# A 4-layer float32 encoder trunk: evictions, squares and a gate's transfer change their place in the heads of the sub-layers

## The chip, the cores and the metric

One Trainium2 chip, 1 core. The metric is the device time of one launch in microseconds, as the median of repeated runs. TensorE has two clock levels, 1.2 and 2.4 GHz; the profile shows which share of the full one was granted.

## The reference, cut to what matters

The input x has 256 tokens of 1024 features, float32. Four layers follow; each has a token mixer (layers 0 and 3: latent attention, called MLA here; layer 1: a convolution module, conv; layer 2: causal pooling) and a squared-ReLU MLP. Every one of these eight sub-layers is wrapped in the same way:

```python
mod = c_act @ ada_w[i] + ada_b[i]
sh_m, sc_m, gt_m, sh_f, sc_f, gt_f = jnp.split(mod, 6, axis=-1)
h = _rmsnorm(x, norm_g[i, 0]) * (1.0 + sc_m[:, None]) + sh_m[:, None]
y = mixer(h)
x = x + gt_m[:, None] * _rmsnorm(y, norm_g[i, 1])
h = _rmsnorm(x, norm_g[i, 2]) * (1.0 + sc_f[:, None]) + sh_f[:, None]
y = jnp.square(jax.nn.relu(h @ w1)) @ w2
x = x + gt_f[:, None] * _rmsnorm(y, norm_g[i, 3])
```

What lies between two sub-layers is called a head here: y of the old one is normed, multiplied by its gate and added to x (the residual), and x is normed, scaled, shifted and transposed for the new one. A head bears the name of the sub-layer that follows it.

## The kernel before

**Work and numbers.** The 256 tokens are two tiles of 128 partitions (tile 0 and tile 1); x stays in SBUF as `xs`. Float32 products are made of three products in the rounded type float32r: a value is split into a high part (ScalarE, a cast) and a low part (VectorE, value less high part), and high x high, high x low and low x high are summed in PSUM. Weights are streamed by SP's queue into five buffers `raw` and split by `load` (lines 160 to 176: the cast on line 173, the subtraction on line 174), activations into two planes `hT`, high and low. The adaLN products `c_act @ ada_w` are spread over the whole kernel in units of a megabyte; `ada` (line 204) issues them on TensorE (line 271, eight matmul records a unit) or as accumulations on VectorE. A finished group becomes a row in `rows`, is staged in DRAM, and is sent back by POOL as a copy on all partitions (`spread`, line 330, the transfer on line 331, 512 KB): `bc_g` is the gate, `bc_a` the scales of the next sub-layer. `gate_row` (line 344) sends a mixer's gate, once for a layer.

**The order of work.** SP's transfers run in the order of the code. All other engines get their order from a planner, which goes by the order of the code, by estimated durations and by what is ready. Instructions that pass through `line(engine, ...)` (line 127) are chained on their engine in just the order in which the code makes them; `after` (line 147) puts the loads that follow a head behind the last instruction of that head on their engine. What passes through neither, such as the loads' casts and subtractions elsewhere, is set by the planner.

**A head** is `boundary` (lines 536 to 599). In the order of the code, each step in line on its engine: TensorE's pending adaLN units (`ada(units)`; from MLP 0's head to MLP 3's there are 1, 1, 2, 4, 1, 0 and 0 of them), squares of y of tile 0 (ScalarE, line 135), the two multiplications of y by the gate (`y_scaled`, VectorE, line 528), sum and power -1/2 of the mean (POOL, lines 119 and 121), residual (line 533), squares of the new x, and its scaling by `bc_a` (`scaled`, line 389). Then for tile 0 `transposed0`: a diagonal of the inverse norm (`dg`, ScalarE, line 403), and for each of two halves of the features one product that lays down the shift (line 395) and transposing products (line 409) into one PSUM bank. Meanwhile tile 1 gets its squares of y, multiplications by the gate, sum on VectorE (line 117), power on POOL, and residual. `fill0` evicts the two banks of tile 0 (lines 571 to 577): the cast into the high plane on ScalarE (line 573), the subtraction into the low plane on VectorE (line 574). Both casts stand in ScalarE's line ahead of tile 1's squares (line 581). Then `first(0)`, tile 0 of the next sub-layer's first block of weights, runs on TensorE (24 matmuls on line 645 in an MLP or in conv, 12 on line 836 in MLA) while tile 1's inverse norm is made; `transposed1` scales tile 1 (`xa`, VectorE, line 420), transposes it (TensorE, line 426), and evicts it in eight pieces (lines 429 and 431). Tile 1 of the first block follows, then chunk 1 of the MLP (line 671).

`headblock` (line 631) makes the first block for an MLP and for conv; its two halves of weights are loaded ahead of the head in the code. It goes through the high plane of all eight feature blocks first, with high and low weights (16 matmuls), and then through the low plane (8). The first half of the features is in the first bank of `fill0`, the second half in the second.

**Pooling** (lines 1266 to 1370) calls the same `boundary` with its own pieces: `tokens` (line 1287) in place of the transposes, and `early` (line 1343), which is called twice: after tile 1's multiplications by the gate, for the means of tile 0, and after tile 1's power. After the head come the rest of its product, `gate_row(i)` and `prep(i, 2)`, which send its own gate and the scales of MLP 2, and at the end one adaLN unit. The subtractions on line 1320 make the low plane of its means; the product on line 1330 needs it. The gate that is sent here is used in the next head, MLP 2's, on line 528.

Of the kernel before, what the change touches and what calls it, by code (L numbers as in the profile page):

```python
# [11 lines left out]
F32 = mybir.dt.float32  # L12
# [4 lines left out]
ALU = mybir.AluOpType  # L17
# [34 lines left out]
def tile_trunk(ctx: ExitStack, tc: tile.TileContext, x, cT, pos, invf, ada_w, ada_bg,  # L52
# [104 lines left out]

    loaded = {}

    def load(src, pre=None, lined=False):  # L160
        key = (src.tensor.name, src.offset)
        if key in loaded:
            return loaded.pop(key)
        o = (slice(0, src.shape[0]), slice(0, src.shape[1]))
        if key not in fetched:
            fetch(src)
        raw = fetched.pop(key)
        if pre is not None:
            pre(raw)
        h = his.tile([P, D], F32R, tag="hi", name="hi")[o]  # L170
        l = los.tile([P, D], F32R, tag="lo", name="lo")[o]
        put = (lambda ins, eng: line(eng, ins)) if lined else after
        put(A.copy(h, raw), "act")  # L173
        put(V.tensor_tensor(l, raw, h.bitcast(F32), op=ALU.subtract), "dve")  # L174
        gate["free"] -= 1
        return h, l

# [355 lines left out]
            line("dve", V.scalar_tensor_tensor(xs[:, t, sl], v, r, xs[:, t, sl],  # L533
                                               op0=ALU.mult, op1=ALU.add))

    def boundary(ys, units, planes=None, tokens=None, early=None, first=None):
        defer[0] = []
        ada(units)
        late, defer[0] = defer[0], None
        last.clear()  # L540
        final = planes is None and tokens is None
        m0, m1 = [sm.tile([P, 2], F32, tag="msy", name="msy") for _ in range(NT)]
        y_squares(0, ys, 0, m0)
        y_squares(0, ys, 1, m0)
        v0 = [y_scaled(0, ys, h) for h in range(2)]
        residual(0, v0, rsqrt_eps(*cols(m0)))
        if final:
            nc.sync.dma_start(out[0], xs[:, 0])
        else:
            ms = squares(0)  # L550
            xa = scaled(0)
        y_squares(1, ys, 0, m1)
        if not final:
            r = rsqrt_eps(*cols(ms))
            if tokens is None:
                bs = transposed0(xa, r)
        v1 = [y_scaled(1, ys, 0)]
        if tokens is not None:
            tokens(xa, r)
        y_squares(1, ys, 1, m1)  # L560
        r1 = rsqrt_eps(*cols(m1), eng=V)
        v1.append(y_scaled(1, ys, 1))
        if tokens is not None:
            low = early()
        if final:
            for v in v1:
                residual(1, [v], r1)
                nc.sync.dma_start(out[1, :, v[0]], xs[:, 1, v[0]])
            return

        def fill0(h):
            o = (slice(None), slice(4 * h, 4 * h + 4), slice(0, P))
            line("act", A.copy(planes[0][o], bs[h]))
            return lambda: line("dve", V.tensor_tensor(
                planes[1][o], bs[h], planes[0][o].bitcast(F32), op=ALU.subtract))
        if tokens is None:
            low = [fill0(h) for h in range(2)]
        residual(1, v1, r1)
        if tokens is not None:
            low[0][0]()  # L580
        ms = squares(1)
        r = rsqrt_eps(*cols(ms))
        if tokens is not None:
            low[1][0]()
            early()
            xa = scaled(1)
            low[0][1]()
            tokens(xa, r)
            low[1][1]()
        else:  # L590
            for l in low:
                l()
            if first is not None:
                first(0)
            transposed1(r, *planes)
        for a in late:
            ada_row(*a, line)
        gate["pool"] = gate["pow"]
        gate["free"] = GFREE if first is None else 0
# [28 lines left out]

    def headblock(src, hh, hl):
        parts = [load(src[p]) for p in range(2)]
        banks = []

        def tile_of(t):
            ts = slice(t * P, (t + 1) * P)
            b = bank("h", "h0")[:, 0:256]
            banks.append(b)
            n = 0
            for low in (False, True):  # L640
                for kk in range(KT):
                    wh, wl = parts[kk // 4]
                    c = slice(256 * (kk % 4), 256 * (kk % 4) + 256)
                    for st, mv in ((hl, wh),) if low else ((hh, wh), (hh, wl)):
                        line("pe", T.matmul(b, st[:, kk, ts], mv[:, c], start=(n == 0),  # L645
                                            stop=(n == 3 * KT - 1), skip_group_check=True))
                        n += 1
        return tile_of, banks
# [617 lines left out]
    def pool(i, head, consts, units, ahead):  # L1266
# [75 lines left out]

        def early():
            if not spilt:
                parts = [means(0, h) for h in range(2)]
                spilt.append(spill(0))
                return parts
            y.extend(y_banks())
            biased(0)
            product(0, 0)  # L1350
# [10 lines left out]
        for _, low in parts:  # L1361
            low()
        gate["free"] = 0
        gate_row(i)
        prep(i, 2)
        biased(1)
        product(1, 0)
# [24 lines left out]
    for s in range(nsub + 1):  # L1392
# [6 lines left out]

        if s == nsub:  # L1400
            boundary(y, 0)
        elif m == 0 and i % 3 == 2:
            y = pool(i, head, consts, sched[0], sched[2])
            pp.close()
        else:
            hi, lo = planes()
            first = None
            if m or i % 3 == 1:
                first = headblock(w1[i, 0] if m else w_pw1[i // 3, 0], hi, lo)
            elif s:  # L1410
                run = downblock(w_dkv[i // 3], hi, lo)
                first = [lambda t: run(t, (0, 1, 2, 3)), run]
            if s == 0:
                start(hi, lo)
                small_loads()
            else:
                head(planes=(hi, lo), first=first and first[0])
            if m:
                if i % 3 == 1:
                    pp = ExitStack()  # L1420
                    pool_p = pp.enter_context(tc.tile_pool(name=f"pool{i + 1}", bufs=1))
                    consts = pool_consts(pool_p, (i + 1) // 3)

                def mid():
                    if i + 1 < DEPTH:
                        prep(i + 1, 0)
                        if (i + 1) % 3 != 2:
                            shift_rows()
                    if i % 3 == 1:
                        spread(consts[2], i + 1, 0, 0)  # L1430
                        shift_rows(rows[(i + 1, 2)])
                y = ffn(i, (hi, lo), sched[0], sched[2], mid, first)
            else:
                args = (i, (hi, lo), sched[0], sched[2])
                if i % 3 == 0:
                    y = mla(*args, first and first[1])
                else:
                    y = conv(*args, first)
# [93 lines left out]
```

## Time and profile before

| what | value |
|---|---|
| median of 3 runs | 1166.6 us (1164.24 to 1167.7) |
| the profiled execution's own time | 1165.46 us |
| its span, first to last instruction | 1163.7 us |
| granted TensorE clock, mean over the span | 0.985 |
| TensorE matmuls busy | 1116.9 us (96%) |
| VectorE busy | 860.2 us (74%) |
| ScalarE busy | 643.3 us (55%) |
| POOL busy | 55.8 us (5%) |
| SP's DMA queue, share of the 16 DMA engines | 66.5% |
| HBM traffic | 248 GB/s over the span |

A row of the profile names an engine (PE is TensorE, PEld its loading of weights, DVE VectorE, ACT ScalarE), the line of the kernel, the operation, and what it writes and reads. An engine that is busy is not always the one that limits; the views that follow show who waits for whom, and when. A timeline joins neighbouring instructions of the same line and tile into one row with their count; the number in brackets is the time for which the engine stood idle before the row, and what released it.

### The profile page before, as it was taken

What the parts mean: (1) busy time and instruction counts of PE and PEld (TensorE: products, weight loads), DVE (VectorE), ACT (ScalarE), POOL (GpSimd) and SP (SyncE); (2) the same over time, 40 slices, a digit from 0 to 9 for tenths busy, and PEclk for the clock granted to TensorE, in tenths of its full rate; (3) what the DMA queues carried; (4) which work ended last, traced back from release to release, by engine and by line L of the source; (5) the groups of instructions that cost most, each with busy time, mean ns of one, the idle gap of its engine ahead of it and who ended that gap; (6) DMA issues with size and microseconds to landing.
All of it is one profiled execution on the core that took longest, in us unless ns stands there. A gap on an engine that the chain in (4) does not pass through costs nothing.

```text
span 1163.7 us, 17551 instructions
## 1 busy us (share of the span) xinstructions
PE 1116.9 (96%) x6682; PEld 910.8 (78%) x6682; DVE 860.2 (74%) x1206; ACT 643.3 (55%) x1146; POOL 55.8 (5%) x129
## 2 busy tenths in 40 slices
PE   7899999999999989999999989999998899999997
PEld 4667778878877767888888768888877778888886
DVE  3789788889675656888876688888756986655554
ACT  3455566555654225655564555656556665655653
POOL 1000000000010001000000100000010001000000
PEclk8999999999999989999999989999998999999999
DMA  9877769987825894898877559988625522765650
GB/s 367 321 275 305 294 241 348 336 318 286 316 86 174 308 341 155 307 388 328 307 282 293 226 207 379 332 314 289 210 72 177 172 91 71 258 197 188 188 187 36
DMA packets 73388, 290.02 MB, mean 249 GB/s; under 512 B 9988, under 2 KB 15236, under 8 KB 61016
## 3 DMA queue, kind: packets, MB, share of 16 engines
q1 hardware_dynamic: 70488, 280.45, 66.5%
q0 software_dynamic: 2816, 8.46, 2.1%
q8 instruction: 52, 0.85, 0.3%
q14 instruction: 32, 0.26, 0.1%
HBM read 286.58 MB, written 2.29 MB: 248 GB/s over the span
## 4 chain that ended last, share of the span: by engine, by line
PE 79%; DVE 7%; DMA 6%; ACT 3%; issue 3%; POOL 2%; SPq 0%; POOLq 0%; DVEq 0%; ACTq 0%
PE h L671 19%; PE y L602 11%; PE y L605 11%; PE y L606 11%; PE h L674 10%; PE adap L271 2%; DMA raw<-in_w_pw_dram 2%; ACT junk L135 2%; PE dw_ps L1131 2%; PE s_ps L1043 1%; DVE lo L174 1%; PE h L645 1%; POOL r L121 1%; PE pw L625 1%; PE pw L619 1%
## 5 line engine op out<-in xcount | busy, mean ns | idle before, releaser
L174 DVE TENSOR_TENSOR lo<-raw,hi 128x1024 fp32r<-128x1024 f32 (+1 forms) x334 | 391.4, 1194 | 79.6 <-ACT hi L173 53.1
L173 ACT CAST hi<-raw 128x1024 fp32r<-128x1024 f32 (+1 forms) x334 | 333.8, 1029 | 67.4 <-PE y L606 32.1
L671 PE MATMUL h<-hT,hi 128*128 128x512 f32 x960 | 240.0, 391 | 0.0
L671 PEld LDWEIGHTS h<-hT,hi 128*128 128x128 f32 x960 | 175.9, 188 | 36.2 <-issue 2.5
L605 PE MATMUL y<-lo,gh 128*128 128x512 f32 x512 | 200.0, 391 | 0.1
L606 PE MATMUL y<-hi,gl 128*128 128x512 f32 x512 | 199.1, 390 | 0.0
L602 PE MATMUL y<-hi,gh 128*128 128x512 f32 x512 | 197.2, 393 | 1.4 <-ACT hi L173 1.4
L736 ACT COPY r<-h 128x256 f32<-128x256 f32 x120 | 44.6, 372 | 183.4 <-PE h L674 183.3
L674 PEld LDWEIGHTS h<-hT,lo 128*128 128x128 f32 x960 | 130.8, 190 | 11.5 <-issue 2.5
L223 DVE SCALAR_TENSOR_TENSOR acc<-araw,c_act,acc 128x1024 f32<-128x1024 f32 x110 | 135.8, 1280 | 0.6 <-DMA araw<-in_ada_w_dram 0.5
L674 PE MATMUL h<-hT,lo 128*128 128x256 f32 x960 | 135.0, 283 | 0.0
L606 PEld LDWEIGHTS y<-hi,gl 128*128 128x128 f32 x512 | 96.1, 188 | 21.0 <-DVE gl L742 0.6
L602 PEld LDWEIGHTS y<-hi,gh 128*128 128x128 f32 x512 | 95.6, 188 | 21.2 <-ACT hi L173 1.6
L605 PEld LDWEIGHTS y<-lo,gh 128*128 128x128 f32 x512 | 96.3, 188 | 20.3 <-issue 1.7
L737 DVE TENSOR_TENSOR r<-h,r 128x256 f32<-128x256 f32 x120 | 50.3, 421 | 44.6 <-ACT r L736 43.5
L742 DVE TENSOR_TENSOR gl<-r,gh 128x512 fp32r<-128x512 f32 x60 | 41.4, 691 | 39.5 <-ACT gh L741 39.1
L738 ACT ACTIVATE r<-r 128x512 f32<-128x512 f32 x60 | 38.0, 633 | 33.3 <-DVE r L737 33.0
L528 DVE TENSOR_TENSOR v<-y,bc_g 128x512 f32<-128x512 f32 x32 | 21.9, 688 | 27.0 <-ACT junk L135 20.3
L602 PE MATMUL y<-hi,hT 128*128 128x512 f32 x96 | 38.2, 399 | 1.3 <-DVE hT L1230 1.3
L739 ACT ACTIVATE r<-r 128x512 f32<-128x512 f32 x60 | 37.9, 632 | 1.6
L741 ACT CAST gh<-r 128x512 fp32r<-128x512 f32 x60 | 37.2, 621 | 1.7
L605 PE MATMUL y<-lo,hT 128*128 128x512 f32 x96 | 37.5, 391 | 0.0
(262 smaller groups left out, 1470.2 us busy)
## 6 DMA issues: line engine op xcount, KB each, us to landing
raw<-in_w_dram SPq DMA_DIRECT2D x256, 512.0 KB, 4.7
araw<-in_ada_w_dram SPq DMA_DIRECT2D x96, 1024.0 KB, 7.2
raw<-in_w_pw_dram SPq DMA_DIRECT2D x24, 512.0 KB, 7.5
raw<-in_w_o_dram SPq DMA_DIRECT2D x16, 512.0 KB, 4.4
u<-ud SPq DMA_DIRECT2D x32, 132.0 KB, 3.3
raw<-in_w_ukv_dram SPq DMA_DIRECT2D x8, 512.0 KB
bc_g<-rowd POOLq DMA_DIRECT2D x8, 512.0 KB, 4.2
bc_a<-rowd POOLq DMA_DIRECT2D x7, 512.0 KB, 8.0
```

The source lines that it names most:

```text
L173: put(A.copy(h, raw), "act")
L174: put(V.tensor_tensor(l, raw, h.bitcast(F32), op=ALU.subtract), "dve")
L223: V.scalar_tensor_tensor(acc, raw[:, sl], ck, acc, op0=ALU.mult, op1=ALU.add)
L602: mm = T.matmul(o, ah, bh, start=start, stop=False, skip_group_check=True)
L605: T.matmul(o, ah, bl, start=False, stop=False, skip_group_check=True)
L606: return T.matmul(o, al, bh, start=False, stop=stop, skip_group_check=True)
L671: T.matmul(b, w(0, kk), pair[:, :, kk], start=(kk == 0), stop=False, skip_group_check=True)
L674: T.matmul(b[:, 0:S], w(1, kk), pair[:, 0, kk], start=False, stop=(kk == KT - 1), skip_group_check=True)
L736: A.copy(rf, hb[:, S:])
L737: V.tensor_tensor(rf, hb[:, 0:S], rf, op=ALU.add)
L738: A.activation(r, r, AF.Relu)
L742: gli = V.tensor_tensor(gl, g2, gh.bitcast(F32), op=ALU.subtract)
```

## The change

In the six heads that are not pooling's, the second bank of tile 0 is evicted by VectorE (a copy) in place of ScalarE, and this copy stands in the code behind tile 1's squares, behind the residual in VectorE's line. Where the head has adaLN units, the first bank's subtraction goes ahead of it; in the other two heads (MLA of layer 3 and MLP 3) the copy goes first. In MLP 2's head alone, the two subtractions of the first block's weights are held back and put in VectorE's line behind the scaling of tile 0. In pooling, `gate_row(i)` moves from behind the head into the first call of `early`.

```diff
--- before.py
+++ after.py
@@ -157,7 +157,7 @@
 
     loaded = {}
 
-    def load(src, pre=None, lined=False):
+    def load(src, pre=None, lined=False, held=None):
         key = (src.tensor.name, src.offset)
         if key in loaded:
             return loaded.pop(key)
@@ -171,7 +171,12 @@
         l = los.tile([P, D], F32R, tag="lo", name="lo")[o]
         put = (lambda ins, eng: line(eng, ins)) if lined else after
         put(A.copy(h, raw), "act")
-        put(V.tensor_tensor(l, raw, h.bitcast(F32), op=ALU.subtract), "dve")
+        def rest():
+            return V.tensor_tensor(l, raw, h.bitcast(F32), op=ALU.subtract)
+        if held is None:
+            put(rest(), "dve")
+        else:
+            held.append(lambda: line("dve", rest()))
         gate["free"] -= 1
         return h, l
 
@@ -533,7 +538,7 @@
             line("dve", V.scalar_tensor_tensor(xs[:, t, sl], v, r, xs[:, t, sl],
                                                op0=ALU.mult, op1=ALU.add))
 
-    def boundary(ys, units, planes=None, tokens=None, early=None, first=None):
+    def boundary(ys, units, planes=None, tokens=None, early=None, first=None, held=()):
         defer[0] = []
         ada(units)
         late, defer[0] = defer[0], None
@@ -549,6 +554,8 @@
         else:
             ms = squares(0)
             xa = scaled(0)
+            for h in held:
+                h()
         y_squares(1, ys, 0, m1)
         if not final:
             r = rsqrt_eps(*cols(ms))
@@ -570,11 +577,14 @@
 
         def fill0(h):
             o = (slice(None), slice(4 * h, 4 * h + 4), slice(0, P))
-            line("act", A.copy(planes[0][o], bs[h]))
+            if h == 0:
+                line("act", A.copy(planes[0][o], bs[h]))
+            else:
+                line("dve", V.tensor_copy(planes[0][o], bs[h]))
             return lambda: line("dve", V.tensor_tensor(
                 planes[1][o], bs[h], planes[0][o].bitcast(F32), op=ALU.subtract))
         if tokens is None:
-            low = [fill0(h) for h in range(2)]
+            low = [fill0(0)]
         residual(1, v1, r1)
         if tokens is not None:
             low[0][0]()
@@ -588,6 +598,9 @@
             tokens(xa, r)
             low[1][1]()
         else:
+            if units:
+                low.pop(0)()
+            low.append(fill0(1))
             for l in low:
                 l()
             if first is not None:
@@ -628,8 +641,8 @@
 
 
 
-    def headblock(src, hh, hl):
-        parts = [load(src[p]) for p in range(2)]
+    def headblock(src, hh, hl, held=None):
+        parts = [load(src[p], held=held) for p in range(2)]
         banks = []
 
         def tile_of(t):
@@ -1342,6 +1355,7 @@
 
         def early():
             if not spilt:
+                gate_row(i)
                 parts = [means(0, h) for h in range(2)]
                 spilt.append(spill(0))
                 return parts
@@ -1361,7 +1375,6 @@
         for _, low in parts:
             low()
         gate["free"] = 0
-        gate_row(i)
         prep(i, 2)
         biased(1)
         product(1, 0)
@@ -1404,9 +1417,10 @@
             pp.close()
         else:
             hi, lo = planes()
-            first = None
+            first = held = None
             if m or i % 3 == 1:
-                first = headblock(w1[i, 0] if m else w_pw1[i // 3, 0], hi, lo)
+                held = [] if m and i % 3 == 2 else None
+                first = headblock(w1[i, 0] if m else w_pw1[i // 3, 0], hi, lo, held)
             elif s:
                 run = downblock(w_dkv[i // 3], hi, lo)
                 first = [lambda t: run(t, (0, 1, 2, 3)), run]
@@ -1414,7 +1428,7 @@
                 start(hi, lo)
                 small_loads()
             else:
-                head(planes=(hi, lo), first=first and first[0])
+                head(planes=(hi, lo), first=first and first[0], held=held or ())
             if m:
                 if i % 3 == 1:
                     pp = ExitStack()
```

## Rows read from the trace of the kernel before

**Rows 1.** Waits of TensorE, whole span: us in total, times, longest us.

```profile
PE hT_ps L426 <- DVE xa L420: 6.6, 11, 1.9
```

**Rows 2.** Timeline, TensorE, 654 to 690: start, us, what, [idle before <-releaser].

```profile
653.79 1.90 PE L271 MATMUL adap<-araw,c_act 128*32 128x512 f32 x16
...
670.48 1.33 PE L1330 MATMUL y<-hi,hT 128*128 128x256 f32 x8 [2.86 <-DVE hT L1320]
671.74 3.61 PE L271 MATMUL adap<-araw,c_act 128*32 128x512 f32 x16
...
677.12 1.16 PE L409 MATMUL hT_ps<-dg,xa 128*128 128x128 f32 x8 [1.36 <-ACT dg L403]
...
683.10 1.12 PE L645 MATMUL h<-hi,hT 128*128 128x256 f32 x8
...
688.93 1.41 PE L671 MATMUL h<-hT,hi 128*128 128x512 f32 x5
```

**Rows 3.** Timeline, VectorE, 654 to 690.

```profile
654.82 0.68 DVE L528 TENSOR_TENSOR v<-y,bc_g 128x512 f32<-128x512 f32 x1
...
668.54 1.29 DVE L528 TENSOR_TENSOR v<-y,bc_g 128x512 f32<-128x512 f32 x2 [6.67 <-DMA bc_g<-rowd]
669.74 1.28 DVE L1320 TENSOR_TENSOR hT<-pT_ps,hT 128x512 fp32r<-128x512 f32 x2
670.94 2.35 DVE L174 TENSOR_TENSOR lo<-raw,hi 128x1024 fp32r<-128x1024 f32 x2
673.21 1.41 DVE L533 SCALAR_TENSOR_TENSOR xs<-v,r,xs 128x512 f32<-128x512 f32 x2
...
678.55 1.41 DVE L533 SCALAR_TENSOR_TENSOR xs<-v,r,xs 128x512 f32<-128x512 f32 x2
```

**Rows 4.** Timeline, POOL, 654 to 690.

```profile
654.98 0.55 POOL L121 TENSOR_TENSOR r<-v,mhalf 128x1 f32<-128x1 f32 x1 [1.86 <-DVE v L117]
...
659.77 0.63 POOL L331 DMA_DIRECT2D bc_g<-rowd  x1
660.40 0.55 POOL L331 DMA_DIRECT2D bc_a<-rowd  x1
```

**Rows 5.** Line 331, whole span: its sends' time to landing.

```profile
DMA to landing us min/median/max: 3.8/5.3/10.5
```

**Rows 6.** Stretches: us, each engine's busy time, PEclk, DMA share, GB/s.

```profile
656.00:659.00 3.00, 3.00 (x25) 2.67 (x24) 2.79 (x5) 2.15 (x6) 0.13 (x1) 1.00 1.00 421
671.00:675.00 4.00, 4.00 (x22) 1.16 (x21) 4.00 (x6) 0.92 (x3) 0.00 (x0) 0.60 0.21 31
```

**Rows 7.** Timeline, ScalarE, 654 to 690.

```profile
663.92 0.19 ACT L135 ACTIVATION_READ_ACCUMULATOR junk<-y 128x1 f32 x1
...
674.05 0.63 ACT L135 ACTIVATE junk<-xs 128x512 bf16<-128x512 f32 x1 [6.66 <-DVE xs L533]
...
676.67 0.40 ACT L403 ACTIVATE dg<-ident,r 128x128 f32<-128x128 f32 x1 [0.42 <-POOL r L121]
```

**Rows 8.** Line 1067: xcount, ns min/median/max, first and last start, shape.

```profile
L1067 DVE COPY ptA<-pT_ps x8: 685/692/693, 83.1 to 955.2; 128x512 f32<-128x512 f32 x8
```

**Rows 9.** Timeline, MLP 3's head, ScalarE, VectorE, TensorE, 973 to 990.

```profile
977.78 0.59 ACT L573 CAST hT<-hT_ps 128x512 fp32r<-128x512 f32 x1 [0.91 <-PE hT_ps L409]
...
976.53 1.42 DVE L533 SCALAR_TENSOR_TENSOR xs<-v,r,xs 128x512 f32<-128x512 f32 x2
...
980.83 1.54 DVE L420 SCALAR_TENSOR_TENSOR xa<-xs,r,bc_a 128x256 f32<-128x256 f32 x3 [1.69 <-POOL r L121]
...
981.37 0.83 PE L426 MATMUL hT_ps<-ident,xa 128*128 128x128 f32 x4 [0.77 <-DVE xa L420]
...
985.93 2.09 PE L671 MATMUL h<-hT,hi 128*128 128x512 f32 x8
```

**Rows 10.** Timeline, TensorE, in the heads of conv and of MLA.

```profile
344.64 0.84 PE L426 MATMUL hT_ps<-ident,xa 128*128 128x128 f32 x4 [1.07 <-DVE xa L420]
...
872.57 0.88 PE L426 MATMUL hT_ps<-ident,xa 128*128 128x128 f32 x4 [1.91 <-DVE xa L420]
```

## The prediction

> **What bounds the kernel now.** The table of the page is read first: TensorE is busy 96% of the span, so a change pays only where TensorE itself stands still, or where a chain that it waits for gets shorter. Its waits come next: eleven for the scaled copy of the second tile, 6.6 us in all, the longest 1.9 [rows 1]; two in each of the six ordinary heads, one in MLP 2's. The third view is the timeline from pooling into MLP 2, where the largest hole is. TensorE stands 2.86 us before a product of pooling, and 1.36 before the transposes of the next head [rows 2]. VectorE stands 6.67 us before its first multiplication by the gate [rows 3]: the gate was sent at 659.77 [rows 4], and that multiplication starts 8.8 us after the send. The order on VectorE makes it worse: the two subtractions of pooling (L1320) for which TensorE waits stand behind the multiplications by the gate, and the residual stands behind two subtractions of weights, 2.35 us for the pair [rows 3]. From 671 to 675 the granted clock was 0.60 [rows 6], a mean between the two levels of 1.2 and 2.4 GHz, right after TensorE had stood; 16 accumulations took 3.61 us there against 1.90 at 653.79 [rows 2].
>
> **Part 1: pooling sends its gate from within its head.** The send now stands on POOL behind the power that ends at 655.53 [rows 4], and its buffer is free when the last multiplication by the old gate ends, at 655.50 [rows 3]. So it goes at 655.6 instead of 659.77. It holds POOL for 0.63 us [rows 4]; what stands behind it there is the second tile's sum and power, which wait for squares that come later, so nobody waits for POOL. On SP's queue nothing moves. On the DMA engines, full at that time (share 1.00, 421 GB/s [rows 6]), the gate's 512 KB go ahead of as much of other loads, which come 1.2 us later; the first that is used feeds the accumulations at 671.74. How long does the gate take? Line 331's sends took between 3.8 and 10.5 us [rows 5]; I take the 8.8 of this very one, since the engines are as full, and both ends for the range. The multiplications by the gate then start at 664.4. They could not start before 664.1, when the squares of y are through [rows 7], so a faster transfer is worth 0.3 us at most, and a slower one (10.5) costs 1.8.
>
> The Trainium skill (DMA: Bandwidth & Descriptors, Anatomy of one DMA) gives such a transfer 2.0 us plus its bytes at 436 GB/s, by estimate 3.2 us for 512 KB. The trace does not agree: 8.8 us beside full engines. By the page the gate would be there at 658.8, and the sum below would be the 0.3 us larger.
>
> From there each step keeps its distance. L1320 starts 1.2 us after the multiplications; its pair, 1.28, ends at 666.9 [rows 3]. TensorE reaches that product at 667.6, so its wait of 2.86 is gone, the product ends at 668.9, and the accumulations, at the full clock's 1.90, at 670.8 [rows 2].
>
> **Part 2: the subtractions of MLP 2's first weights are held.** They leave their place ahead of the residual. That now starts 1.2 us after L1320, at 666.8 instead of 673.21 [rows 3]: 6.4 us, of which 4.1 are the gate's and 2.3 the pair's. The first tile's diagonal follows 3.46 us later as it did (676.67 after 673.21 [rows 3, 7]), at 670.3. With one shift product of some 0.4 after 670.8 the transposes start at 671.2 instead of 677.12, without their wait. The pair now stands ahead of the second tile. The row of scales, sent at 659.8 (now 660.40 [rows 4]), is there by the same 8.8 at 668.6; the scaling by it (1.2), the pair (2.35), and the two multiplications by the gate (1.29) bring the second tile's residual to 673.5 instead of 678.55. The first matmul that needs the held subtractions comes after the transposes, and they end at 672.1 (now 673.3), so neither TensorE nor SP's next loads into those buffers wait longer.
>
> **Part 3: the second eviction goes to VectorE, in six heads.** On ScalarE it took 0.59 us [rows 9], and the second tile's squares stood behind it. No row shows VectorE copying from PSUM into the rounded type. The like copy of 128x512 from PSUM takes it 0.692 [rows 8]; I take 0.69, with ScalarE's 0.59 as the other end. On VectorE it stands behind the residual (1.42) and, in a head that has accumulations, behind the first subtraction too (0.64, half of the pair's 1.28). Who waits for it: 16 of the 24 matmuls of the first block's tile.
> - MLP 3. The squares could start 0.84 after the residual's start (as 674.05 after 673.21 [rows 3, 7]), at 977.4; now they follow the eviction that ends at 978.4 [rows 9]. The second half's square follows 0.75 behind the first, so the scaled copy comes 0.9 earlier, 979.9 instead of 980.83. But VectorE's copy ends at 978.6, ScalarE's at 978.4: the block's tile ends 0.2 later, at 980.8 (now 981.37 less the wait of 0.77 [rows 9]). The transposes follow at once. In MLP 2, where they do so today, chunk 1 begins 4.7 us after that tile's end (688.93 after 684.22 [rows 2]). So 985.5 instead of 985.93: 0.4 us.
> - MLA. TensorE waits 1.91 us [rows 10], and its first block uses the first half alone, so the copy delays nothing: 0.85, about MLP 3's 0.9.
> - Conv. The wait is 1.07 [rows 10]; an accumulation that stands ahead of the scaled copy takes part of it: 0.5.
> - MLP 0 and 1 have accumulations, so the copy comes 0.64 later and TensorE waits for it in place of the scaled copy: 0.2 each, between -0.4 and 0.8.
> - MLP 2. Residual from 673.5 to 674.9, subtraction, copy: 676.3. The other 16 matmuls take 2.1 (8 in 1.12 [rows 2]): 678.4. With 4.7 more, chunk 1 starts at 683.1 instead of 688.93: 5.8 us, for all three parts.
>
> **Sum.** 5.8 + 0.4 + 0.85 + 0.5 + 0.4 = 8.0 us. From the profiled execution's 1165.46 this gives 1157.5; that execution lies 1.1 below the median of the runs shown, so 1158.6. Behind the heads the MLPs go at TensorE's pace, so what a head gains stays. With the slow transfer 5.8 becomes 4.0; if the other heads lose 0.4 each, or all waits of rows 1 go, their 2.2 becomes -2.0 or some 5. Ends: 1164.6 and 1155.5.
>
> **Rivals.**
> - The heads give nothing: VectorE becomes what TensorE waits for. For it speaks that the copy ends later there in five heads; against it, that in MLA nothing else waits. Then pooling's 5.8 less up to 0.6 is left: 1161.
> - The gate lands late. A send of line 331 has taken 10.5 us [rows 5]. Mechanism: right behind the new send VectorE works without a pause on residual and scaling, and POOL's descriptors are written later. The gate is used from 666.2, L1320 ends at 668.7, and TensorE waits 1.1: 1.8 us are lost, 1160.4. The Trainium skill (SBUF — State Buffer, SBUF: two separate sides) says that VectorE's two-port modes keep POOL from writing descriptors; no run here shows whether such a mode is at work.
> - The gate does not go early: its issue stays where it is on POOL, because the planner so orders it. Then only the held pair pays, 2.3, and the heads up to 2.2: 1162 to 1164.5. Against it: from 655.53 on POOL has nothing to do before the second tile's sum.
> - Slower. The planner orders the unlisted casts, subtractions and accumulations by its own estimate of times. Moved heads may set a subtraction of weights ahead of what TensorE needs, on VectorE, in the stages behind the first head. Each place costs 1.2 us, half of the pair's 2.35 [rows 3]; of 64 chunks more than seven have to be hit before the gain is gone. With ten: 1170.
>
> **How the numbers follow.** The forecast's case has 0.58, the heads' rival 0.16, the late gate 0.08, the gate not early 0.12, slower 0.06. A measurement of this kernel can tell about 0.3%, 3.5 us, from no change. The first three are faster by more, and so is a quarter of the fourth, the rest of which lies within: 0.85, 0.09, 0.06. The range goes from 1155.0, all waits of the heads gone, to 1163.5, which takes in half of the fourth case.
>
> **What would show it.** The gate is sent at 655.6 and used at 664.4; TensorE does not wait at 667.6; the residual of MLP 2 starts at 666.8, its chunk 1 at 683.1 (earlier by what the heads before have gained). In the other heads the squares stand right behind the first eviction, and in place of the wait before the second transposes there are short waits for VectorE's copy. The prediction is wrong if the gate is used after 666, if a wait for the row of scales takes its place, or if chunk 1 in MLP 3 follows its head no sooner than today.

## The result and the profile after

The changed kernel takes 1158.72 us in the median (1156.78 to 1160.32, 5 runs), the kernel before 1165.72 on the same chip (1163.28 to 1167.70, 5 runs): ratio 0.9939, 95% interval 0.9920 to 0.9958. Measured twice more, it gave 0.9933 (0.9912 to 0.9954) and 0.9932 (0.9911 to 0.9954). The forecast was 1158.6, with a range of 1155.0 to 1163.5, and faster; so the total is right. Its parts are not: in the trace pooling's passage gave 2.58 us of the 5.8 that were forecast (some 70% in two later traces), the other heads twice as much as forecast.

In the profile after, TensorE's waits for the second tile's scaled copy are down from 6.6 us in eleven [rows 1] to 1.3 in four. The wait for the diagonal in MLP 2's head has grown from 1.36 [rows 2] to 2.05; the other of the two in the first row, some 0.6 in MLA's head, stood there before too. TensorE's waits from 140 to 1000 us (total, times, longest):

```profile
PE hT_ps L414 <- ACT dg L408: 2.7, 2, 2.1
...
PE hT_ps L431 <- DVE xa L425: 1.3, 4, 0.7
```

The passage from pooling into MLP 2 follows, engine by engine (timelines of the kernel after: start, us, what, idle before). First GpSimd, which answers to [rows 4]:

```profile
655.10 0.63 POOL L336 DMA_DIRECT2D bc_g<-rowd  x1 [0.27 <-DVE v L533]
...
669.45 1.58 POOL L119 TENSOR_SCALAR v<-ms 128x1 f32<-128x1 f32 x1 [4.99 <-ACT junk L135]
671.12 1.39 POOL L121 TENSOR_TENSOR r<-v,mhalf 128x1 f32<-128x1 f32 x1
```

VectorE, which answers to [rows 3]:

```profile
664.73 1.29 DVE L533 TENSOR_TENSOR v<-y,bc_g 128x512 f32<-128x512 f32 x2 [3.56 <-DMA bc_g<-rowd]
665.94 0.74 DVE L538 SCALAR_TENSOR_TENSOR xs<-v,r,xs 128x512 f32<-128x512 f32 x1
666.60 1.28 DVE L1333 TENSOR_TENSOR hT<-pT_ps,hT 128x512 fp32r<-128x512 f32 x2
667.80 0.74 DVE L538 SCALAR_TENSOR_TENSOR xs<-v,r,xs 128x512 f32<-128x512 f32 x1
668.52 1.29 DVE L394 TENSOR_TENSOR xa<-xs,bc_a 128x512 f32<-128x512 f32 x2
669.73 2.35 DVE L175 TENSOR_TENSOR lo<-raw,hi 128x1024 fp32r<-128x1024 f32 x2
```

And TensorE, which answers to [rows 2]:

```profile
667.34 1.33 PE L1343 MATMUL y<-hi,hT 128*128 128x256 f32 x8 [0.41 <-DVE hT L1333]
668.60 1.92 PE L276 MATMUL adap<-araw,c_act 128*32 128x512 f32 x16
...
672.99 1.97 PE L414 MATMUL hT_ps<-dg,xa 128*128 128x128 f32 x8 [2.05 <-ACT dg L408]
...
675.61 2.07 PE L414 MATMUL hT_ps<-dg,xa 128*128 128x128 f32 x8
...
685.66 1.56 PE L684 MATMUL h<-hT,hi 128*128 128x512 f32 x6
```

The gate does go early, the wait of 2.86 before pooling's product shrinks to 0.41, and the accumulations run at the full clock (1.92 where 3.61 stood). Then GpSimd's sum (line 119) and power (line 121) of the first tile take 1.58 and 1.39 us. In the kernel before they took 0.37 and 0.56:

```profile
675.62 0.37 POOL L119 TENSOR_SCALAR v<-ms 128x1 f32<-128x1 f32 x1 [10.46 <-ACT junk L135]
676.07 0.56 POOL L121 TENSOR_TENSOR r<-v,mhalf 128x1 f32<-128x1 f32 x1
```

The diagonal waits for them, TensorE for the diagonal, and behind that wait the clock falls: both groups of transposes take some 2 us, and the stretches from 674 on show half of the full clock (us, busy time by engine, granted clock, DMA share, GB/s):

```profile
674.00:676.00 2.00, 2.00 (x8) 1.34 (x8) 1.94 (x4) 1.01 (x2) 0.39 (x1) 0.50 1.01 414
676.00:678.00 2.00, 2.00 (x11) 2.00 (x11) 0.72 (x2) 0.92 (x4) 0.87 (x3) 0.50 0.85 346
678.00:680.00 2.00, 2.00 (x11) 2.00 (x11) 1.97 (x5) 0.00 (x0) 0.56 (x1) 0.51 0.32 82
```

The first chunk of MLP 2 comes at 685.66. From the start of the accumulations to it are 17.06 us, where the kernel before took 17.19 (688.93 less 671.74 [rows 2]): nearly all that was won lies ahead of them.

**Where the time went, head by head.** Each of TensorE's matmuls was set against the same one, in order of issue, in the trace of the kernel before; a passage's gain is the change, across it, of the median distance between the two starts. In us, for all kernels of this study:

| kernel | pooling to MLP 2 | MLP 0 | conv | MLP 1 | MLA | MLP 3 | five heads |
|---|---|---|---|---|---|---|---|
| forecast | 5.8 | 0.2 | 0.5 | 0.2 | 0.85 | 0.4 | 2.2 |
| after | 2.58 | 0.55 | 0.70 | 1.19 | 1.24 | 0.75 | 4.4 |
| after, again | 4.25 | 0.43 | 0.69 | 1.19 | 0.42 | 0.78 | 3.5 |
| after, third | 4.11 | 0.87 | 0.70 | 1.21 | 0.78 | 0.78 | 4.3 |
| gate only | 4.14 | -0.05 | 0.05 | 0.03 | 0.03 | 0.01 | 0.1 |
| eviction only | -0.49 | 0.48 | 0.70 | 1.20 | 1.06 | 0.78 | 4.2 |
| squares first | -0.23 | 0.73 | 0.96 | 0.97 | 0.88 | 0.38 | 3.9 |
| no held pair | 5.51 | 0.62 | 0.65 | 1.21 | 0.99 | 0.80 | 4.3 |
| held later | 5.66 | 0.88 | 0.70 | 1.20 | 0.85 | 0.78 | 4.4 |
| held later, again | 5.83 | 0.56 | 0.70 | 1.21 | 0.65 | 0.79 | 3.9 |
| PSUM work instead | 2.91 | 0.64 | 0.71 | 1.21 | 1.14 | 0.77 | 4.5 |
| later, ScalarE's copy | 6.09 | 0.57 | 0.68 | 1.21 | 0.86 | 0.79 | 4.1 |
| mixed | 5.97 | 0.34 | 0.97 | 1.21 | 1.04 | 0.79 | 4.4 |

Outside the heads single executions differ by as much. By 135 us every one of these runs is 1.4 to 5.0 us behind the profiled execution of the kernel before, and inside conv each gains 1.1 to 4.4, "gate only" 3.1 of it with conv's code untouched. Neither belongs to the change.

### The profile page after: what moved, and what is told of

Same layout as the page of the kernel before. It is cut to its first block, busy times and chain, and to the rows that moved or that the text cites. A ratio compares the mean times of both kernels' runs of the same rounds, so it can differ in the third digit from the quotient of the medians.

```text
span 1157.0 us, 17554 instructions
## 1 busy us (share of the span) xinstructions
PE 1114.3 (96%) x6682; PEld 913.4 (79%) x6682; DVE 864.2 (75%) x1212; ACT 639.2 (55%) x1140; POOL 58.4 (5%) x129
## 4 chain that ended last, share of the span: by engine, by line
PE 80%; DVE 6%; DMA 6%; ACT 3%; issue 2%; POOL 2%; SPq 0%; POOLq 0%; DVEq 0%; ACTq 0%
PE h L684 19%; PE y L615 11%; PE y L618 11%; PE y L619 11%; PE h L687 10%; PE adap L276 2%; PE h L658 2%; DMA raw<-in_w_pw_dram 2%; PE dw_ps L1144 1%; ACT junk L135 1%; PE s_ps L1056 1%; DVE lo L175 1%; POOL r L121 1%; PE pw L632 1%; PE pw L638 1%
## 5 line engine op out<-in xcount | busy, mean ns | idle before, releaser
L533 DVE TENSOR_TENSOR v<-y,bc_g 128x512 f32<-128x512 f32 x32 | 21.9, 688 | 22.4 <-ACT junk L135 18.7
```

## The experiments

In the passage into MLP 2 these are the numbers that tell the kernels apart (us, from the timelines; the last column runs from the start of the sixteen accumulations to that of the first chunk):

| kernel | GpSimd's sum | power | TensorE waits for the diagonal | transposes, 1st and 2nd group | to chunk 1 |
|---|---|---|---|---|---|
| before | 0.37 | 0.56 | 1.36 | 1.16, 2.07 | 17.19 |
| after | 1.58 | 1.39 | 2.05 | 1.97, 2.07 | 17.06 |
| after, again | 1.57 | 1.39 | 2.04 | 1.16, 2.08 | 15.52 |
| after, third | 1.67 | 1.39 | 2.15 | 1.16, 2.06 | 15.63 |
| gate only | 1.44 | 0.85 | 1.38 | 1.16, 2.07 | 15.66 |
| no held pair | 1.44 | 0.85 | 1.38 | 1.16, 1.16 | 14.02 |
| held later | 0.67 | 0.56 | 0.32 | 1.16, 1.16 | 14.15 |
| held later, again | 0.55 | 0.56 | under 0.3 | 1.16, 1.16 | 14.15 |
| PSUM work instead | 0.55 | 0.56 | 2.16 | 1.16, 1.99 | 16.84 |
| later, ScalarE's copy | 0.67 | 0.56 | 0.32 | 1.16, 1.16 | 13.81 |
| mixed | 0.50 | 0.56 | under 0.3 | 1.16, 1.16 | 13.80 |

**1. The early gate alone** (kernel before, lines of `pool`):

```diff
             if not spilt:
+                gate_row(i)
                 parts = [means(0, h) for h in range(2)]
...
         gate["free"] = 0
-        gate_row(i)
         prep(i, 2)
```

> The kernel before with pooling's gate sent from within its head, and nothing else. Theory A (after the change, GpSimd's sum and power for the diagonal took 1.58 and 1.39 us because the held pair of subtractions ran beside them, and this took back what holding the pair brought): VectorE does gate multiplication, eviction pair, weight pair, residual, scaling one behind the other from about 665.4, the diagonal starts near 673.7 where it was at 676.67, both GpSimd instructions take under 1 us together with 0.4, and the first chunk of MLP 2 comes 2.5 to 3.5 us earlier relative to the work ahead of it, about what the whole change gave there (2.6). Theory B (the held pair earned its 2.35 us as forecast, and the loss was elsewhere): the early gate alone gives 0.3 us or nothing. Total: A 1163 us, B 1165.5 us.

Measured: 1161.13 us, ratio 0.9959 (0.9943 to 0.9974). The passage gives 4.14 us, the two GpSimd instructions take 1.44 and 0.85, and the diagonal starts at 672.11. So the gate gave by itself what theory A gave it and 0.6 us beyond its range: the planner set the residual ahead of the weights' pair by itself, its first half even ahead of pooling's subtractions, so the diagonal came 1.6 us sooner than expected, though GpSimd's two instructions, expected under 1 us, were slow here too (the pair, not held, ran beside them). Theory B falls.

**2. The eviction and the squares alone** (the diff's lines in `fill0` and the four behind it, on the kernel before):

```diff
-            line("act", A.copy(planes[0][o], bs[h]))
+            if h == 0:
+                line("act", A.copy(planes[0][o], bs[h]))
+            else:
+                line("dve", V.tensor_copy(planes[0][o], bs[h]))
...
-            low = [fill0(h) for h in range(2)]
+            low = [fill0(0)]
...
+            if units:
+                low.pop(0)()
+            low.append(fill0(1))
```

> The kernel before with the second eviction on VectorE and the second tile's squares ahead of it in every head, the gate where it was. Theory A: what the heads gave after the change is theirs: TensorE's work moves up by 0.55 (MLP 0), 0.7 (conv), 1.2 (MLP 1), 1.1 (MLA) and 0.76 us (MLP 3), 4.3 in sum, and something between 0 and 1 us in MLP 2's head; total about 1161 us. Theory B (the forecast's own: 0.2, 0.5, 0.2, 0.85, 0.4): 2.2 us in sum, total 1163.5 us, the rest of the heads' gain after the change being chance of one profiled execution.

Measured: 1160.62 us, ratio 0.9947 (0.9931 to 0.9964). Head by head theory A's sizes repeat within 0.1, 4.2 us in all. In MLP 2's head, where 0 to 1 us of gain was expected, it loses 0.49; the clock was at the half level for about 10 us there, where the kernel before had about 7 (worked out from the mean clocks of the stretches, 655 to 685).

**3. The held pair one place later on VectorE** (kernel after):

```diff
             xa = scaled(0)
-            for h in held:
-                h()
...
         v1 = [y_scaled(1, ys, 0)]
+        for h in held:
+            h()
```

> The kernel after the change with the held pair one place later on VectorE, behind the multiplication of the second tile's first half by the gate. Theory A (GpSimd's instruction cannot run beside a VectorE instruction that reads two operands from SBUF): the sum takes 0.4 us instead of 1.58 and the power 0.6 to 1.0 instead of 1.39, the diagonal starts near 670.7 instead of 672.54, TensorE's wait of 2.05 us ahead of the transposing products falls under 0.4, and the first chunk of MLP 2 comes 1.5 to 3 us earlier than after the change; total 1156 to 1157.5 us. Theory B (the two GpSimd instructions are slow for another reason, such as the DMA issues or the clock): they still take 2.5 us or more together and the time stays at 1158.7 us.

Measured: 1156.11 us, ratio 0.9912 (0.9899 to 0.9925). GpSimd and VectorE in the timeline of this kernel:

```profile
669.09 0.67 POOL L119 TENSOR_SCALAR v<-ms 128x1 f32<-128x1 f32 x1 [4.83 <-ACT junk L135]
669.85 0.56 POOL L121 TENSOR_TENSOR r<-v,mhalf 128x1 f32<-128x1 f32 x1
```

```profile
668.30 1.29 DVE L394 TENSOR_TENSOR xa<-xs,bc_a 128x512 f32<-128x512 f32 x2
669.75 0.69 DVE L533 TENSOR_TENSOR v<-y,bc_g 128x512 f32<-128x512 f32 x1 [0.15 <-ACT junk L135]
670.36 2.35 DVE L175 TENSOR_TENSOR lo<-raw,hi 128x1024 fp32r<-128x1024 f32 x2
```

The same pair, 0.6 us later, and GpSimd is back to 0.67 and 0.56. The sum began at 669.09 (its time includes any wait beside VectorE) and ended at 669.77, 0.18 after the scaling (L394), whose two operands lie in SBUF, had ended at 669.59 (668.30 plus 1.29). The power ran beside L533, one of whose operands lies in PSUM, at its usual 0.56. TensorE:

```profile
670.89 1.16 PE L414 MATMUL hT_ps<-dg,xa 128*128 128x128 f32 x8 [0.32 <-ACT dg L408]
...
672.39 1.16 PE L414 MATMUL hT_ps<-dg,xa 128*128 128x128 f32 x8
676.16 0.39 PE L658 MATMUL h<-hi,hT 128*128 128x256 f32 x1 [1.66 <-DVE hT L583]
...
682.39 1.78 PE L684 MATMUL h<-hT,hi 128*128 128x512 f32 x7
```

No half clock, and chunk 1 is 5.66 us earlier than in the kernel before: the forecast's 5.8, without the delay. Theory A holds. A new wait shows, 1.66 us for VectorE's copy.

**4. PSUM work in the pair's place** (on the kernel of experiment 3; the results of the three multiplications are not used):

```diff
             xa = scaled(0)
+            if held:
+                v = tmp.tile([P, 512], F32, tag="v", name="v", bufs=3)
+                for h in (0, 1, 0):
+                    line("dve", V.tensor_tensor(v, ys[1][h], bct["g"][:, HALF[h]],
+                                                op=ALU.mult))
```

> As the kernel with the held pair later, but in the place the pair left stand three multiplications of 128x512 (2.1 us) with one operand in PSUM and one in SBUF, whose results are not used. Theory A (two SBUF operands on VectorE block GpSimd): the sum takes about 0.4 us and the power 0.57, the diagonal starts near 670.6. Theory B (any busy VectorE slows GpSimd): the two take 2.5 us or more together, as after the change. In both the second tile's residual is some 2 us later than with the pair moved.

It ran once (1159.45 us), so its time is not compared. GpSimd, VectorE and ScalarE in its timeline:

```profile
668.14 0.55 POOL L119 TENSOR_SCALAR v<-ms 128x1 f32<-128x1 f32 x1 [4.88 <-ACT junk L135]
668.77 0.56 POOL L121 TENSOR_TENSOR r<-v,mhalf 128x1 f32<-128x1 f32 x1
```

```profile
668.43 2.21 DVE L560 TENSOR_TENSOR v<-y,bc_g 128x512 f32<-128x512 f32 x3
```

```profile
670.75 0.60 ACT L135 ACTIVATE junk<-y 128x512 bf16<-128x512 f32 x1 [2.71 <-DVE v L560]
...
671.34 0.39 ACT L408 ACTIVATE dg<-ident,r 128x128 f32<-128x128 f32 x1
```

VectorE works without a pause from 668.43 to 670.64, and the power that runs beside it takes 0.56. A busy VectorE alone does not slow GpSimd; theory B falls. The diagonal missed its 670.6: the power was ready at 669.33, but the square of y that stands ahead of the diagonal on ScalarE waited 2.71 us for the added multiplications, which read the same PSUM tiles. That delay is this experiment's own.

**5. Held later, and in MLP 2's head the second copy on ScalarE, ahead of the squares:**

```diff
-            if h == 0:
+            if h == 0 or held:
                 line("act", A.copy(planes[0][o], bs[h]))
...
-            low = [fill0(0)]
+            low = [fill0(h) for h in range(2 if held else 1)]
...
-            if units:
-                low.pop(0)()
-            low.append(fill0(1))
+            if not held:
+                if units:
+                    low.pop(0)()
+                low.append(fill0(1))
```

> As the kernel with the held pair later, but in MLP 2's head alone both evictions of the first tile are on ScalarE again, ahead of the second tile's squares. Theory A (there ScalarE stands idle for 1.66 us when the second bank is ready at 673.55, while VectorE's copy has to wait behind the residual until 675.43): TensorE's wait of 1.7 us for VectorE's copy goes, the second tile's scaled copy becomes the limit, and the first chunk of MLP 2 comes 0.5 to 1 us earlier than with VectorE's copy; total about 1155.4 us. Theory B (the copy on VectorE is as good there as in the other heads): no change within 0.3 us or up to 0.7 us later, 1156.1 us or more.

Measured: 1155.84 us, ratio 0.9927 (0.9906 to 0.9949). From the accumulations to chunk 1 it takes 13.81 where experiment 3 took 14.15, a gain of 0.34. The wait of 1.66 for the copy is gone, but about half of it comes back as waits for the scaled copy (0.53 and 0.25 us), and the second tile's transposes, now in two groups, take 0.90 and 0.63 instead of 1.04. Between the two theories' sizes.

**6. After without the held pair:**

```diff
-                held = [] if m and i % 3 == 2 else None
```

> The kernel after the change without the held pair: the two subtractions stand where the planner puts them, between the residual and the scaling. Theory A (holding the pair back, where the change puts it, costs more than it brings, since it then runs beside GpSimd's power as well): the power takes 0.85 us instead of 1.39, the diagonal starts 0.3 to 0.6 us earlier and the first chunk of MLP 2 comes 0.5 to 1.2 us earlier than after the change; total 1157.5 to 1158.5 us. Theory B (the forecast's: holding the pair brings 2.3 us): the chunk comes 2 us later, total 1161 us.

Measured: 1155.38 us, ratio 0.9918 (0.9894 to 0.9942), with "after, again", measured together with it, at 1157.23; the intervals of the two ratios overlap. The planner puts the pair between residual and scaling, 668.70 to 671.05 in "gate only" and likewise here:

```profile
668.85 1.44 POOL L119 TENSOR_SCALAR v<-ms 128x1 f32<-128x1 f32 x1 [5.10 <-ACT junk L135]
670.37 0.85 POOL L121 TENSOR_TENSOR r<-v,mhalf 128x1 f32<-128x1 f32 x1
```

VectorE's rows beside them:

```profile
667.85 2.35 DVE L175 TENSOR_TENSOR lo<-raw,hi 128x1024 fp32r<-128x1024 f32 x2
670.12 1.28 DVE L394 TENSOR_TENSOR xa<-xs,bc_a 128x512 f32<-128x512 f32 x2
```

The sum is nearly as slow, the power less so, and TensorE waits 1.38 us instead of 2.05. The power stands beside the scaling alone, 128x512 with both operands in SBUF, and takes 0.85; beside experiment 4's multiplications, 128x512 too but with one operand in PSUM, it took 0.56. So it is not the length of VectorE's instruction that tells. Holding the pair back where the change holds it does not bring 2.3 us; it costs 0.7 (2.05 less 1.38), and in this execution the clock's fall as well. Theory A on the sign, beyond its range on the size (1.5 us to chunk 1 against "after, again"; 3.0 against the first trace). Against experiment 3 nothing is lost at chunk 1: 14.02 here, 14.15 there.

**7. Squares first, the copy stays on ScalarE behind them** (as experiment 2, without the copy on VectorE).

> The kernel before with the second tile's squares ahead of the second eviction, which stays on ScalarE, behind them. Theory A (the heads' gain comes from the squares going first, not from the engine of the copy): the five ordinary heads together gain as with the copy on VectorE, 4.2 us (0.5, 0.7, 1.2, 1.05, 0.78) within 1 us, total about 1161 us. Theory B (the copy must also leave ScalarE): the copy, now behind the squares, makes TensorE wait for it as long as it waited for the scaled copy; the heads gain under 2 us, total 1164 us or more.

Measured: 1160.33 us, ratio 0.9961 (0.9942 to 0.9981). The five heads give 3.9 us, against 4.2. It is the order that pays. The engine of the copy matters by head: VectorE's is better by 0.4 in MLP 3 and 0.2 in MLP 1, ScalarE's by 0.26 in conv.

**8. The kernel after, once more.**

> The kernel after the change, once more, as a yardstick beside the three others. Theory A (what differs between two profiled executions in the first 30 us and between 400 and 435 us is chance of the clock): the work up to 135 us is not 4.4 us later than in the kernel before, but anything between 0 and 5; the passage from pooling into MLP 2 and the heads repeat within 0.3 us, GpSimd's sum at 1.58 and its power at 1.39 us. Theory B (the change moves the start): the 4.4 us repeat. Total 1158.7 us within 1.5 in both.

Measured: 1157.23 us. GpSimd's two instructions repeat to 0.01, the wait is 2.04, but the passage gives 4.25 instead of 2.58, since the clock fell later and for less long; the start is 3.8 us behind that of the kernel before, where "eviction only" was 1.4 behind. MLA's head gave 0.42 instead of 1.24. So of theory A the 0.3 us does not hold for the passage and MLA's head. On the start 3.8 lies near theory B's 4.4 too; what decides is "gate only", 2.8 behind with the code ahead of pooling untouched.

**9. Mixed:** held later; the second copy on ScalarE behind the squares in MLP 0 and conv, on ScalarE ahead of them in MLP 2, on VectorE elsewhere (in the kernel of experiment 5, `h == 0 or units == 1`).

> The held pair later, and the second eviction by head: on ScalarE behind the squares in MLP 0 and conv, on ScalarE ahead of them in MLP 2, on VectorE in MLP 1, MLA and MLP 3 (each where the runs so far gave most). Theory A (the parts add up): pooling into MLP 2 gains 6 us or more against the kernel before, MLP 0 0.7, conv 0.95, MLP 1 1.2, MLA 0.9 to 1.1, MLP 3 0.78, 10.5 us in all; ratio near 0.991. Theory B (a head takes back what another gives, through the clock or the planner's order): under 9 us.

Measured: 1152.79 us, ratio 0.9902 (0.9871 to 0.9933), the lowest median of the study. In its trace the passage and the five heads give 5.97 and 4.35, 10.3 us together; MLP 0 gave 0.34 where 0.7 was expected. TensorE goes through the passage almost without a stand:

```profile
667.78 1.16 PE L414 MATMUL hT_ps<-dg,xa 128*128 128x128 f32 x8
...
669.28 1.16 PE L414 MATMUL hT_ps<-dg,xa 128*128 128x128 f32 x8
...
679.10 2.08 PE L685 MATMUL h<-hT,hi 128*128 128x512 f32 x8
```

**10 and 11. Held later and after, again.**

> The kernel with the held pair later, once more, beside the one after the change in the same call. Theory A (TensorE's wait ahead of the transposes stays under 0.5 us, and so the clock does not fall behind it): the sixteen accumulations to the first chunk of MLP 2 take 14.1 us again, 1.4 to 2.9 less than after the change, the granted clock is 1.00 all the way, and the median is 1 to 3 us below that of the kernel after the change. Theory B (the clock's fall there is chance whatever TensorE does): 15 to 17 us, and no difference in the medians.

> The kernel after the change for the third time. TensorE's wait for the diagonal is 2.0 to 2.1 us again, GpSimd's two instructions 1.6 and 1.4; by theory A the clock falls to 0.50 behind that wait again, for 3 to 6 us, and the accumulations to the first chunk take 15.5 to 17.1 us; by theory B it may as well not fall (14 us).

Measured together: 1155.67 us (0.9920, 0.9896 to 0.9944) and 1158.22 (0.9932). To chunk 1: 14.15, exactly as in experiment 3, and 15.63. The medians differ by 2.6 us, within theory A's 1 to 3, though the intervals of the ratios overlap, so by the times alone the difference is not shown. In three executions of the kernel after, the clock fell three times, and it was at half speed for about 7 us once and for 3.4 us twice (worked out from the mean clocks of the stretches); with the pair later it never did in two.

## Why the prediction was right in sum and wrong in parts

- **The gate.** It was sent as predicted. It was used 9.6 us after the send (664.73 less 655.10), not 8.8: between the value taken and the end kept for the range (10.5 [rows 5]). That is 0.8 of the 2.9 us by which the diagonal came late (next point). Pooling's subtractions started 1.87 us after the multiplications (666.60 less 664.73), not 1.2, since the planner set the first half of the residual between them; with the later gate that left 0.41 of TensorE's wait. The rival of the late gate happened by half.
- **The held pair: the step that failed.** "The first tile's diagonal follows 3.46 us later as it did (676.67 after 673.21 [rows 3, 7]), at 670.3." The stage runs 0.7 us ahead, so 669.6 was forecast, and 672.54 was measured. 3.46 was a distance across GpSimd, taken over from a place where VectorE did other work, and the pair was then put beside just those two instructions: 1.58 and 1.39 us instead of 0.37 and 0.56, 2.0 us. Experiment 3 moves only the pair and gets them back; experiment 4 shows that it is not VectorE's being busy. Where the pair stood next, and who ran beside it there, was not asked of the step that moved it. Nor were the pair's 2.3 us there to be won: once the gate is early, the planner sets the pair behind the residual by itself ("gate only", "no held pair"). Held later, the pair gives hardly more than not held: 5.66 and 5.83 against 5.51 in the passage, and 14.15 against 14.02 to chunk 1, since what the diagonal's wait gives (0.32 for 1.38) the wait for VectorE's copy takes back (1.66 for 0.49).
- **The mechanism.** Wherever the sum or the power is slow in this passage, it ends 0.1 to 0.5 us behind a VectorE instruction with both operands in SBUF: here the sum at 671.03, 0.1 after the pair's first half, the power at 672.51, 0.4 after the second. Beside multiplications that read PSUM it keeps its 0.3 to 0.6. The Trainium skill (SBUF — State Buffer, SBUF: two separate sides) says so: a VectorE instruction with two SBUF inputs and a GpSimd instruction that reads SBUF share a port pair that one of them holds for its whole instruction; the other is blocked. The trace agrees: 1.58 and 1.39 us beside the pair, 0.55 and 0.56 beside experiment 4's multiplications. The prediction took from that section only the sentence that bears on descriptors, and missed this one, which spoke against the pair's new place.
- **The clock.** The forecast had the transposes at 1.16 us, since TensorE would not stand. It stood 2.05, and the stretches behind show 0.50. That the stand brought the fall is argued from its place in time; the last section names stands that no fall followed. Three executions of one kernel lost different amounts by it (17.06, 15.52, 15.63 to chunk 1), so of the missing 3.2 us (5.8 less 2.58) some 1.5 are one execution's chance; the other two gave 4.25 and 4.11.
- **MLP 2's head.** The forecast counted the copy on VectorE as part of its gain. It costs 0.34 us, between experiments 3 and 5, both at the full clock. ScalarE stands idle there when the bank is ready (673.55 in experiment 3), while VectorE is at the residual and copies from 675.43. The 0.49 lost in experiment 2 cannot be put down to the copy, since the clock was at the half level longer there; squares first, with the copy on ScalarE, loses 0.23 as well.
- **The other heads: 2.2 forecast, 3.5 to 4.4 measured.** The squares did go first, and most of the waits went, from 6.6 us to 1.3. (They are two in each of five ordinary heads and one in MLP 2's; the prediction's "six" does not add up to eleven.) Two terms were too small, as MLP 1 shows. TensorE in the kernel before and in the one after:

```profile
469.68 1.12 PE L645 MATMUL h<-hi,hT 128*128 128x256 f32 x8
471.55 0.83 PE L426 MATMUL hT_ps<-ident,xa 128*128 128x128 f32 x4 [0.75 <-DVE xa L420]
472.61 0.66 PE L426 MATMUL hT_ps<-ident,xa 128*128 128x128 f32 x4 [0.22 <-DVE xa L420]
...
476.12 1.18 PE L671 MATMUL h<-hT,hi 128*128 128x512 f32 x4
```

```profile
470.28 1.12 PE L658 MATMUL h<-hi,hT 128*128 128x256 f32 x8
471.24 1.04 PE L431 MATMUL hT_ps<-ident,xa 128*128 128x128 f32 x8
...
475.46 1.77 PE L684 MATMUL h<-hT,hi 128*128 128x512 f32 x7
```

From the end of the tile's products to chunk 1 it is 5.32 us before (476.12 less 470.80) and 4.06 after (475.46 less 471.40); the forecast took 4.7, MLP 2's of before, where the transposes too went in two groups with a wait between. Once the scaled copy is early, all eight go in one group of 1.04 us. And the copy was to come 0.64 later, behind the first subtraction; VectorE's rows say otherwise:

```profile
467.60 0.69 DVE L584 TENSOR_TENSOR hT<-hT_ps,hT 128x512 fp32r<-128x512 f32 x1 [0.81 <-ACT hT L581]
468.48 0.69 DVE L583 CAST hT<-hT_ps 128x512 fp32r<-128x512 f32 x1 [0.19 <-PE hT_ps L414]
```

The subtraction runs while TensorE still fills the second bank, and the copy then waits for TensorE. Its 0.69 us is the price taken from [rows 8]. The rival that the heads give nothing is out; so is "slower": no head lost but MLP 2's.
- **The sum.** 5.8 + 2.2 = 8.0 was forecast; 2.58 + 4.43 = 7.0, 4.25 + 3.51 = 7.8 and 4.11 + 4.34 = 8.5 were measured, and by the medians 7.0 to 7.7. Two errors of opposite sign cancelled; that the total came out is luck. The total would not have shown it; chunk 1 of MLP 2, which the prediction named as a mark, did.

What stays open: why the clock falls behind one wait and not behind another as long, why its fall behind the same wait lasts 3.4 us in two executions and about 7 in another, and why "eviction only" gained 5.5 us by the medians where its heads give 3.7 in the trace; its interval reaches down to 4.2.

## What to carry to other kernels

When an instruction is moved, ask who runs beside it at the new place, not only who stands behind it on its queue: a pair of subtractions cost 2 us beside two tiny GpSimd instructions, and no such wait 0.6 us later. An engine's short instructions deserve a look for outliers: one at twice its usual time shows the collision before it matters (in the trace of before GpSimd's sum takes 0.61 us at 342.80, beside an accumulation of 128x1024 on VectorE, and 0.30 in the median). And where several gains are summed, check each at its own mark, since a right total can hide two wrong terms.

## What had not been expected of the hardware

- GpSimd's 128x1 sum took 0.29 to 0.32 us free, 0.35 to 0.67 where it began during a scaling (128x512, both operands in SBUF), and 1.44 to 1.67 where VectorE ran subtractions of 128x1024 with both operands in SBUF beside it. A waiting GpSimd instruction can miss the change from one such instruction of VectorE to the next: the sum that began at 669.45, during the scaling, ended at 671.03, behind the pair's first half. It does not always: in "gate only" the power, begun at 671.22 beside the first half of the scaling, ended at 672.07, before the second half was through (672.26).
- The same happens in conv's head with the copy on VectorE (the power takes 1.42 us beside an accumulation), and costs no wait there: the scaled copy that needs the power starts at 347.22, right behind VectorE's own subtraction.
- In the kernels with the early gate TensorE's clock fell to 0.50 behind waits of 2.04 to 2.16 us in four executions of four, behind 1.38 in one of two, and behind 0.32 or less in none of four. The length of a wait alone does not tell: in the two executions with the pair held later TensorE stood 1.66 and 1.78 us for VectorE's copy, and every stretch behind shows 1.00. With the late gate the clock fell behind 2.86 and 2.55 us, and not behind 2.75 ("squares first", whose accumulations took 1.93).
